# A two-layer diffusion backbone on one core: adaLN bias on rows, feed-forward sums added from PSUM, and the odd mixer's output product begun inside its last attention

## The chip, the cores and the metric

The kernel runs on one core of a Trainium2 chip. The metric is device time in microseconds, lower being better. A core has five engines that run in parallel, each through its own list of instructions in order: TensorE (PE, matrix products and transposes into PSUM), VectorE (DVE), ScalarE (ACT), GpSimd (POOL) and SyncE (SP, which here only issues DMAs). They wait for one another by semaphores.

## The reference

512 latent tokens and 256 context tokens, model width 1024, go through two layers. Each layer is a mixer and a gated feed-forward network, each with adaLN around it and a LayerNorm behind its residual sum:

```python
mod = (c_act @ mod_w[li] + mod_b[li])          # and modc for the context
sh_a, sc_a, g_a, sh_f, sc_f, g_f = jnp.split(mod, 6, -1)
h = x * (1 + sc_a) + sh_a
y = even_mixer(h, hc, ...) if li % 2 == 0 else odd_mixer(h, hc, ...)
x = layer_norm(DEEP_ALPHA * x + g_a * y, ln_g[li, 0], ln_b[li, 0])
hf = x * (1 + sc_f) + sh_f
x = layer_norm(DEEP_ALPHA * x + g_f * conv_ffn(hf, ...), ln_g[li, 1], ln_b[li, 1])
# even mixer's end
dn  = rms_norm(o_dn) * norm_w * silu(z)        # 4 gated DeltaNet heads
ret = group_norm(o_ret) * silu(g)              # 4 retention heads
y = concat([dn, ret]) @ w_out
# odd mixer's end, 8 heads of differential attention
o = rms_norm(softmax(q1 k1) v - lam * softmax(q2 k2) v) * subln_w * (1 - lambda_init)
y = merge_heads(o) @ w_out
```

The context passes through layer 0 with its own modulation; in layer 1 only the latent tokens are carried on.

## The kernel before

Tokens lie on partitions in tiles of 128: four of latent tokens (0 to 3) and two of context (4, 5). To keep float32 accuracy each product is three matmuls, of a high and a low part of either side: xh·wh, xh·wl, xl·wh. A weight comes in *units* of 1024 x 256 (`unit`, L174): SP loads it into `raw` (two buffers), ACT copies the high part `whi` (L147), and POOL or DVE, by `lo_engs`, subtracts to get `wlo` (L148). `raw` multiplied by a gate (L185) is POOL's, too.

A scheduler turns the program into one list per engine, by data dependences and by priority numbers: work written under a large number (`LATE`, 200) fills gaps; `pin` keeps an instruction at its place in program order. Buffers are reused through pools, and an instruction waits until its buffer is free.

The stages in order: the modulation of group 0 and the start; the DeltaNet phase, into which side work is laid (projections of later heads by `fill_unit`, and the adaLN products `mod_group_g`, one step each `SIDE` = 20 ticks); the retention phase (`ret_phase`), in which sums `wacc` of the even output product already run, head by head; `out_proj_ln(l=0)`; `ffn(0)`; the odd mixer; `out_proj_ln(l=1)`; `ffn(1)`.

What the change touches:

- `mod_group_g` multiplies in two halves of eight steps and copies the sum `mod_ps` to `modr` (L367), transposes it (`modt_ps`) and adds the bias `modbT` in columns (L375). `gate_rows` (L1223) reads a gate as rows from memory and adds a row of `mod_b` on POOL (L1232).
- `L1055` scales a DeltaNet head's `o_dn` by its rms `y` and the norm weight `nw`, on DVE, six times for each of four heads.
- In `ret_phase` heads' `kT` are copied by ACT (L1122), and the last head's `hTl` (L1108) is on DVE, behind the split of the last two units.
- At the end of `ffn(0)` each of six tiles gets two halves: gate product `gt` on DVE (L1425), sum into `acc` on POOL or DVE (L1559), LayerNorm, and `hTl` (L148) for the odd mixer.
- The odd mixer takes its heads in four pairs. In `attend` four blocks of queries per head give scores `sc`, probabilities `pt` (L1701, L1709), transposes `aT_ps` and `oall`; each head ends with rms and scaling by `sub` on DVE (L1731). Between, `project` for the next pair is laid in as filling; its rotary sums `otok` (L1618) are on POOL and are transposed by PE into `oT_ps`. In the last pair the filling is `sums` over heads 0 to 5, for tiles 0 and 1 and the first 512 columns, in the PSUM accumulators `accs`; the other two tiles' accumulators start behind the attention.
- `out_proj_ln(l=1)` loads x into `lx`, applies the LayerNorm weights that layer 0 left out (L1358 on DVE, L1359 on POOL), and adds the sums (L1380, L1381, L1383).

## Time and profile before

| | |
|---|---|
| median of three runs | 2055.08 us (2047.45 to 2055.61) |
| the profiled execution | 2056.78 us, of which the trace spans 2055.0 |
| PE busy in it | 1940.2 us, 94% of the span |
| DVE, ACT, POOL busy | 1199.5, 721.6, 765.1 us |
| mean granted clock of PE | 0.975 of full speed |

PE's share tells how much can be gained by any order of the same products; the list of its waits tells where. The clock that was granted to PE is told for each stretch: 1.00 is 2.4 GHz, 0.50 is 1.2 GHz.

### The profile page before, as it was taken

Reading aid. Unit: us, or ns where it says so; the run is one execution under the profiler, and the core shown is the slowest. Engines: PE = TensorE matmul, PEld = TensorE weight load, DVE = VectorE, ACT = ScalarE, POOL = GpSimd, SP = SyncE. Lnnn points to the kernel's source line nnn. Section 1 sums busy time; section 2 is a strip of 40 time slices with the busy share of each in tenths; the row PEclk is TensorE's granted clock in tenths of the full one; section 3 lists DMA queues with packets and bytes.
Section 4 is the critical chain, followed back from the end, with each engine's and each line's share of the span. In section 5 each row is a group of like instructions: output and inputs, shape, how many; then the busy total and the mean of one; then the engine's idle time right before and its main releaser. Section 6 shows DMA issues by size and latency. Waiting matters only on the chain. (4 is left out here: it accounts for less than half of the span.)

```text
span 2055.0 us, 33529 instructions
## 1 busy us (share of the span) xinstructions
PE 1940.2 (94%) x13766; PEld 1674.1 (81%) x13766; DVE 1199.5 (58%) x2452; ACT 721.6 (35%) x1295; POOL 765.1 (37%) x416
## 2 busy tenths in 40 slices
PE   7998999999899999999999998999997989999997
PEld 5877777778888888888888887989886888888886
DVE  3334744443467685666665657366667687656557
ACT  4432343423334432222222225354554444323221
POOL 1232322122422244544454434122213027656571
PEclk9999999999899999999999999999998999999999
DMA  9455344455614231111111112010102233323221
GB/s 290 137 168 163 111 128 141 122 163 181 195 47 164 83 103 62 62 62 62 62 62 62 62 62 90 22 42 30 54 32 78 77 121 126 102 83 103 82 82 41
DMA packets 198113, 201.33 MB, mean 98 GB/s; under 512 B 21336, under 2 KB 186808, under 8 KB 197960
## 3 DMA queue, kind: packets, MB, share of 16 engines
q1 hardware_dynamic: 195832, 196.78, 30.6%
q10 hardware_dynamic: 2128, 2.41, 0.4%
q8 instruction: 108, 1.77, 0.4%
q14 instruction: 45, 0.37, 0.1%
HBM read 185.89 MB, written 13.27 MB: 97 GB/s over the span
## 5 line engine op out<-in xcount | busy, mean ns | idle before, releaser
L148 POOL TENSOR_TENSOR wlo<-raw,whi 128x512 fp32r<-128x512 f32 (+2 forms) x158 | 413.9, 2642 | 487.6 <-ACT whi L147 442.5
L1476 DVE SCALAR_TENSOR_TENSOR ac<-g_ps,fconvT,ac 128x441 f32<-128x441 f32 (+2 forms) x352 | 243.9, 694 | 200.6 <-ACT ac L1465 190.9
L147 ACT CAST whi<-raw 128x2048 fp32r<-128x2048 f32 (+2 forms) x183 | 201.3, 1137 | 389.7 <-issue 247.4
L115 PE MATMUL d_ps<-whi,hh 128*128 128x512 f32 x440 | 173.3, 394 | 5.1 <-DVE gt L1425 4.4
L115 PE MATMUL d_ps<-wlo,hh 128*128 128x512 f32 x440 | 172.2, 391 | 0.0
L115 PE MATMUL d_ps<-whi,hl 128*128 128x512 f32 x440 | 171.6, 391 | 0.0
L115 PE MATMUL opj<-whi,hTh 128*128 128x256 f32 x512 | 147.1, 287 | 2.1 <-ACT oq L1629 1.6
L115 PE MATMUL g_ps<-hTl,whi 128*128 128x512 f32 (+1 forms) x384 | 145.2, 378 | 3.2 <-POOL hTl L148 3.2
L115 PE MATMUL opj<-whi,hTl 128*128 128x256 f32 x512 | 145.9, 285 | 0.0
L115 PE MATMUL opj<-wlo,hTh 128*128 128x256 f32 x512 | 145.1, 283 | 0.0
L115 PE MATMUL g_ps<-hTh,whi 128*128 128x512 f32 (+1 forms) x384 | 144.7, 377 | 0.0
L115 PE MATMUL u_ps<-hTh,whi 128*128 128x512 f32 (+1 forms) x384 | 144.6, 377 | 0.0
L115 PE MATMUL u_ps<-hTh,wlo 128*128 128x512 f32 (+1 forms) x384 | 144.6, 377 | 0.0
L115 PE MATMUL u_ps<-hTl,whi 128*128 128x512 f32 (+1 forms) x384 | 144.5, 376 | 0.0
L115 PE MATMUL g_ps<-hTh,wlo 128*128 128x512 f32 (+1 forms) x384 | 144.4, 376 | 0.0
L115 PE MATMUL fpj<-whi,hTh 128*128 128x256 f32 x432 | 127.1, 294 | 1.1 <-ACT fo L717 1.1
L115 PE MATMUL fpj<-wlo,hTh 128*128 128x256 f32 x432 | 126.7, 293 | 0.0
L115 PE MATMUL fpj<-whi,hTl 128*128 128x256 f32 x432 | 125.2, 290 | 0.0
L115 PEld LDWEIGHTS d_ps<-whi,hh 128*128 128x128 f32 x440 | 82.6, 188 | 26.1 <-DVE gt L1425 7.3
L115 PEld LDWEIGHTS opj<-whi,hTh 128*128 128x128 f32 x512 | 97.5, 191 | 4.2 <-ACT oq L1629 2.6
L1425 DVE TENSOR_TENSOR gt<-d_ps,gate 128x512 f32<-128x512 f32 x120 | 81.7, 686 | 29.7 <-PE d_ps L115 28.8
L115 PE MATMUL c_ps<-hTh,wlo 128*128 128x256 f32 x352 | 98.9, 281 | 0.0
(461 smaller groups left out, 4989.4 us busy)
## 6 DMA issues: line engine op xcount, KB each, us to landing
mraw<-in_mod_w_dram SPq DMA_DIRECT2D x80, 512.0 KB
raw<-in_f_w_gate_dram SPq DMA_DIRECT2D x22, 1024.0 KB
raw<-in_f_w_up_dram SPq DMA_DIRECT2D x22, 1024.0 KB
raw<-in_f_w_down_dram SPq DMA_DIRECT2D x22, 1024.0 KB
raw<-in_o_w_qkv_dram SPq DMA_DIRECT2D x12, 1024.0 KB
raw<-in_e_w_in_dram SPq DMA_DIRECT2D x9, 1024.0 KB
mraw<-in_mod_w_dram SPq DMA_DIRECT2D x32, 256.0 KB
raw<-in_e_w_in_dram SPq DMA_DIRECT2D x8, 512.0 KB
```

Of the source, the lines that this page charges most:

```text
L115: self.nc.tensor.matmul(out, lhsT=lhsT, rhs=rhs, start=start, stop=stop)
L147: self.nc.scalar.copy(h, r)
L148: lo_eng.tensor_sub(l, r, h.bitcast(F32))
L1425: v.tensor_mul(gt, ps, gates[0 if t < NLT else 1][:, n * 512:(n + 1) * 512])
L1476: v.scalar_tensor_tensor(out=o, in0=pv[:, r0 + di:r1 + di, c0 + dj:c1 + dj], scalar=cw[(di + 1) * 3 + dj + 1], in1=o, op0=ALU.mult, op1=AL ...
```

## The change

*adaLN bias.* `SIDE` becomes 18. `mod_group_g` loads four rows of `mod_b`, each spread over 32 partitions, into `modr` ahead of its second half, and adds the product to it from PSUM. The gates that go to memory then hold their bias, and `gate_rows` only loads.

*Even mixer's end.* `nw` is a column; it goes into the first four 128-row blocks of w_out when the unit is split (`unit_out`), and `o_dn`'s scaling is an ACT instruction. The split of the first two units comes after the first retention head's first step; that head's `kT` copies are on DVE.

*First feed-forward end.* The gate product is written back to PSUM, and DVE adds it from there, for all twelve halves. `cparts = 4` stands around the odd mixer's first two units. The projections' plain copies in `fill_unit` use another buffer for tile 2.

*Odd mixer.* x with the postponed LayerNorm weights is made in 16 pieces of 64 columns, during pairs 0 to 2, with two places for a piece (`xa` with `gb`, and `gate0`): loads one attention step ahead, two POOL instructions, a store. All four w_out units are scaled on POOL by gate rows that hold the subln weight. Head scaling is on ACT, the rms chain stays in PSUM. In the last pair `early` sums heads 0 to 5 for all eight blocks (four tiles, two halves) and adds each to ALPHA·x; only heads 6 and 7 are left for the end, which is now written in `odd_mixer` itself.

```diff
-SIDE = 20
+SIDE = 18
...
+    def unit_out(self, src, raw=None, pin=lambda ins: ins):
...
+        for sl, w in ((slice(0, n), self.nw[:, 0:1]), (slice(n, 2 * n), 1.0)):
+            pin(nc.scalar.activation(hi[:, sl], raw[:, sl], AF.Copy, scale=w))
+            pin(nc.vector.scalar_tensor_tensor(out=lo[:, sl], in0=raw[:, sl], scalar=w, in1=hi[:, sl].bitcast(F32),
+                                               op0=ALU.mult, op1=ALU.subtract))
...
+                if (hf, k) == (1, 0):
+                    for j in range(4):
+                        b = a["mod_b"][l, (4 * g + j) * 512:(4 * g + j + 1) * 512]
+                        nc.sync.dma_start(out=modr[32 * j:32 * j + 32, :], in_=b.partition_broadcast(32))
...
-        nc.vector.tensor_copy(modr, ps)
+        nc.vector.tensor_add(modr, ps, modr)
+        yield
...
-            v.scalar_tensor_tensor(out=od, in0=od, scalar=y[:, c:c + 1], in1=self.nw, op0=ALU.mult, op1=ALU.mult)
+            s_.activation(od, od, AF.Copy, scale=y[:, c:c + 1])
...
-                    s_.copy(t[:, grp[0] * P:(grp[-1] + 1) * P], ps[:, :len(grp) * P])
+                    (s_.copy if h or key == "q" else v.tensor_copy)(
+                        t[:, grp[0] * P:(grp[-1] + 1) * P], ps[:, :len(grp) * P])
...
-            self.pin(self.nc.gpsimd.tensor_add(t, t, gb))
...
+                if in_place:
+                    v.tensor_mul(ps, ps, gates[0 if t < NLT else 1][:, n * 512:(n + 1) * 512])
+                if gated or in_place:
                     return acc[t][:, n * 512:(n + 1) * 512], ps
...
-                            (v if n or not key else g).tensor_add(o, o, gt)
+                            v.tensor_add(o, o, gt)
...
+                        s_.activation(oall[:, t, hc], oall[:, t, hc], AF.Copy, scale=r[:, t:t + 1])
...
+                def early(heads):
+
+                    for n in range(2):
+                        for t in range(NLT):
+                            ps = pj.tile([P, 512], F32, tag="wo", name="wo_ps")
+                            with self.priority(LATE):
+                                for h in heads:
+                                    self.out_part([(t, ps)], us[2 * n:2 * n + 2], h, h == heads[-1])
...
+                                for o, c0, n_ in rest(t, n):
+                                    v.scalar_tensor_tensor(out=o, in0=o, scalar=ALPHA, in1=ps[:, c0:c0 + n_],
+                                                           op0=ALU.mult, op1=ALU.add)
...
+                def x_affine(i):
+
+                    cs = slice(i * 64, (i + 1) * 64)
+                    xp, gp = px[(i + 1) % 2]
+                    for j, op in enumerate((g.tensor_mul, g.tensor_add)):
+                        self.pin(op(xp, xp, gp[:, j].unsqueeze(1).to_broadcast([P, NLT, 64])))
+                    nc.sync.dma_start(out=self.xd[2][:LAT, cs].rearrange("(t p) n -> p t n", p=P), in_=xp)
...
+                    if 0 < i <= 16:
+                        x_affine(i - 1)
+                    if i < 16:
+                        x_load(i)
...
+                    if i == 20:
+                        scale(0)
+                        gate_rows_scale(xaf)
+                    if i == 21:
+                        split(0)
...
+                    if i == 23:
+                        scale(1)
+                        scale(2)
...
+                        fill = early(range(6))
...
+                            for h in (6, 7):
+                                self.out_part([(t, ps)], us[2 * n:2 * n + 2], h, h == 7, first=6)
+                            for o, c0, n_ in rest(t, n):
+                                v.tensor_add(acc[t][:, n * 512 + c0:n * 512 + c0 + n_], ps[:, c0:c0 + n_], o)
```

Three places show what this does to the order of work. First, DVE at the even mixer's last head, where `hTl` is what PE's last sums wait for. Before:

```order
L136 SCALAR_TENSOR_TENSOR rs_y<-rs_w,rs_y 128x6
L1207 TENSOR_TENSOR gvar<-gmv,rs_y 128x6
L1208 TENSOR_SCALAR gvar<-gvar 128x6
L148 TENSOR_TENSOR wlo<-raw,whi 128x1024 x4
L1108 TENSOR_TENSOR hTl<-yT_ps,hTh 128x256
L1108 TENSOR_TENSOR hTl<-yT_ps,hTh 128x512
L1385 TENSOR_TENSOR gy<-wacc,gate_7254 128x512 x2
L1386 SCALAR_TENSOR_TENSOR gy<-lx,gy 128x512 x2
```

After:

```order
L149 SCALAR_TENSOR_TENSOR rs_y<-rs_w,rs_y 128x6
L1253 TENSOR_TENSOR gvar<-gmv,rs_y 128x6
L1254 TENSOR_SCALAR gvar<-gvar 128x6
L1152 TENSOR_TENSOR hTl<-yT_ps,hTh 128x256
L1152 TENSOR_TENSOR hTl<-yT_ps,hTh 128x512
L1396 TENSOR_TENSOR gy<-wacc,gate_7266 128x512
L222 SCALAR_TENSOR_TENSOR wlo<-raw,nw,whi 128x1024
L222 SCALAR_TENSOR_TENSOR wlo<-raw,whi 128x1024
```

The two `hTl` and a gate product have moved ahead of the four splits `wlo`.

Second, POOL in the odd mixer's pairs 0 to 2, where `otok` is the rotary sum, `wlo` the split of a unit, and `xa` and `gate` are the two places for pieces of x. Before:

```order
L1618 TENSOR_TENSOR otok<-otok,ob 128x512 x4
L148 TENSOR_TENSOR wlo<-raw,whi 128x2048
L1618 TENSOR_TENSOR otok<-otok,ob 128x512 x2
L148 TENSOR_TENSOR wlo<-raw,whi 128x2048
L1618 TENSOR_TENSOR otok<-otok,ob 128x512 x2
L148 TENSOR_TENSOR wlo<-raw,whi 128x2048 x2
L1618 TENSOR_TENSOR otok<-otok,ob 128x512 x2
```

After, the corresponding first half:

```order
L1634 TENSOR_TENSOR otok<-otok,ob 128x512 x4
L161 TENSOR_TENSOR wlo<-raw,whi 128x2048
L1634 TENSOR_TENSOR otok<-otok,ob 128x512 x2
L1805 TENSOR_TENSOR gate_12984<-gate_12984 128x256
L161 TENSOR_TENSOR wlo<-raw,whi 128x2048
L1805 TENSOR_TENSOR gate_12984<-gate_12984 128x256
L1634 TENSOR_TENSOR otok<-otok,ob 128x512
L1805 TENSOR_TENSOR xa<-xa,gb 128x256 x2
L1805 TENSOR_TENSOR gate_12984<-gate_12984 128x256 x2
L1805 TENSOR_TENSOR xa<-xa,gb 128x256 x2
L1805 TENSOR_TENSOR gate_12984<-gate_12984 128x256
L1634 TENSOR_TENSOR otok<-otok,ob 128x512
```

The pieces, in pairs of instructions, stand between the splits and the rotary sums.

Third, DVE at the odd mixer's end, behind the last head's rms. Before, `hTl` for heads 6 and 7 stands behind the scaling of `oall`, and the affine of `lx` among the sums:

```order
L136 SCALAR_TENSOR_TENSOR rs_y<-rs_w,rs_y 128x4
L1731 SCALAR_TENSOR_TENSOR oall<-oall,rs_y,sub 128x128 x4
L1741 TENSOR_TENSOR hTl<-yT_ps,hTh 128x512 x2
L1380 TENSOR_TENSOR gt<-wo_ps,gate_15588 128x512 x2
L1358 TENSOR_TENSOR lx<-lx,lng 128x1024
L148 TENSOR_TENSOR wlo<-raw,whi 128x1024
L1358 TENSOR_TENSOR lx<-lx,lng 128x1024 x2
L1381 TENSOR_TENSOR lx<-gt,lx 128x512
L1358 TENSOR_TENSOR lx<-lx,lng 128x1024
L1254 BN_STATS lst<-lx 128x6
L1381 TENSOR_TENSOR lx<-gt,lx 128x512
L1383 TENSOR_TENSOR lx<-wo_ps,lx 128x512
```

After, with the late ones of the early sums (L1769) among the sums of heads 6 and 7 (L1914):

```order
L131 SCALAR_TENSOR_TENSOR rs_y<-rs_w,aT_ps 128x4
L1756 TENSOR_TENSOR hTl<-yT_ps,hTh 128x512
L1914 TENSOR_TENSOR oall<-wo_ps,oall 128x512
L1291 BN_STATS lst<-oall 128x6
L1914 TENSOR_TENSOR oall<-wo_ps,oall 128x256
L1769 SCALAR_TENSOR_TENSOR oall<-oall,wo_ps 128x256
L1914 TENSOR_TENSOR oall<-wo_ps,rest 128x256
L1769 SCALAR_TENSOR_TENSOR rest<-rest,wo_ps 128x256
L1291 BN_STATS lst<-oall 128x6
```

The scaling of `oall` and the affine of x have left this place; two halves of an early sum still stand in it.

## Rows read from the trace of the kernel before

**Rows 1.** the page's head: span, busy time of each engine (share of span, instructions).

```profile
span 2055.0 us, 33529 instructions
...
PE 1940.2 (94%) x13766; PEld 1674.1 (81%) x13766; DVE 1199.5 (58%) x2452; ACT 721.6 (35%) x1295; POOL 765.1 (37%) x416
```

**Rows 2.** PE's waits: tile, line, waited for: us in total, times, longest.

```profile
PE ln_ps L119 <- ACT acc L1274: 9.7, 6, 4.3
PE wo_ps L115 <- DVE hTl L1741: 7.4, 1, 7.4
...
PE mod_ps L115 <- DMA mraw<-in_mod_w_dram: 6.0, 4, 3.3
PE wo_ps L115 <- DVE lx L1383: 5.2, 1, 5.2
PE wacc L115 <- DVE hTl L1108: 4.8, 1, 4.8
PE modt_ps L119 <- DVE modr L367: 4.6, 3, 3.3
...
PE rT_ps L119 <- ACT kT L1122: 3.0, 1, 3.0
...
PE oT_ps L119 <- POOL otok L1618: 3.0, 8, 1.0
```

**Rows 3.** windows: start:end, length, busy us (instructions) by engine, PEclk, DMA share, GB/s.

```profile
516.20:523.00 6.80, 5.83 (x28) 5.84 (x29) 2.30 (x10) 2.08 (x9) 1.34 (x4) 0.50 0.58 192
...
635.70:642.50 6.80, 3.72 (x17) 3.72 (x18) 5.92 (x9) 0.00 (x0) 0.00 (x0) 0.50 0.79 253
1267.10:1270.50 3.40, 2.98 (x14) 2.98 (x15) 0.54 (x1) 2.79 (x6) 3.40 (x1) 0.51 0.47 186
1567.50:1570.90 3.40, 3.40 (x17) 3.26 (x17) 3.37 (x6) 1.50 (x3) 2.33 (x1) 0.50 0.92 291
1574.30:1584.60 10.30, 4.32 (x18) 4.13 (x19) 7.55 (x11) 5.36 (x7) 6.87 (x2) 0.50 0.00 0
1618.70:1622.10 3.40, 3.40 (x19) 3.40 (x17) 0.43 (x1) 0.59 (x1) 0.00 (x0) 0.50 0.00 0
1652.80:1659.70 6.90, 5.84 (x27) 5.84 (x28) 6.90 (x18) 1.87 (x3) 0.00 (x0) 0.51 0.00 0
```

**Rows 4.** DVE instructions by line: shortest/median/longest in ns, first and last start.

```profile
L1055 DVE SCALAR_TENSOR_TENSOR o_dn<-o_dn,rs_y,nw x24: 343/346/4637, 278.7 to 511.1; 128x128 f32<-128x128 f32 x24
...
L148 DVE TENSOR_TENSOR hTl<-hf,hTh x16: 674/682/3515, 664.9 to 1679.9; 128x512 fp32r<-128x512 f32 x16
...
L1731 DVE SCALAR_TENSOR_TENSOR oall<-oall,rs_y,sub x32: 337/346/4544, 1359.9 to 1626.8; 128x128 f32<-128x128 f32 x32
...
L148 DVE TENSOR_TENSOR wlo<-raw,whi x25: 691/1220/3410, 11.2 to 1690.2; 128x1024 fp32r<-128x1024 f32 x18, 128x2048 fp32r<-128x2048 f32 x4, 128x512 fp32r<-128x512 f32 x3
```

**Rows 5.** timeline, DVE and POOL: start, us, instruction, [idle before, releaser].

```profile
509.83 5.96 DVE L1055 SCALAR_TENSOR_TENSOR o_dn<-o_dn,rs_y,nw 128x128 f32<-128x128 f32 x6
...
510.92 4.72 POOL L148 TENSOR_TENSOR wlo<-raw,whi 128x2048 fp32r<-128x2048 f32 x1 [4.55 <-ACT whi L147]
...
629.40 8.99 DVE L148 TENSOR_TENSOR wlo<-raw,whi 128x1024 fp32r<-128x1024 f32 x4 [4.48 <-POOL o_ret L1099]
...
629.33 5.71 POOL L1232 TENSOR_TENSOR gate<-gate,gy 128x1024 f32<-128x1024 f32 x2
...
1256.40 4.60 POOL L148 TENSOR_TENSOR wlo<-raw,whi 128x2048 fp32r<-128x2048 f32 x1 [0.42 <-ACT whi L147]
...
1568.58 8.99 POOL L185 TENSOR_TENSOR raw<-raw,gate 128x2048 f32<-128x2048 f32 x2 [11.64 <-DMA raw<-in_o_w_out_dram]
```

**Rows 6.** windows as in group 3: one pair of heads, and the odd end.

```profile
1366.00:1447.00 81.00, 78.71 (x608) 74.39 (x608) 48.78 (x106) 39.53 (x79) 18.79 (x7) 0.98 0.12 40
...
1562.00:1670.00 108.00, 88.14 (x638) 83.39 (x637) 84.35 (x162) 45.28 (x89) 31.06 (x9) 0.89 0.26 85
```

**Rows 7.** POOL's groups by shape: busy us, mean ns, idle before and releaser.

```profile
L713 POOL TENSOR_TENSOR fo<-fo,fb 128x256 f32<-128x256 f32 x16 | 11.9, 744 | 40.3 <-DVE fb L712 27.0 <-issue 5.7 <-DMA XZ<-gdr 4.0
```

More of the change, by code (lines that the diff above doesn't have):

```diff
@@ L174, in unit, with unit_load @@
     def unit(self, parts, scale=None):
+        raw = self.unit_load(parts)
+        if scale is not None:
+            self.unit_scale(raw, scale)
+        return self.unit_split(raw)
+    def unit_load(self, parts):
         nc = self.nc
@@ L296, in setup @@
         nc.vector.memset(self.onescol, 1.0)
+        self.nw = cp.tile([P, 1], F32, name="nw")
+        nc.scalar.dma_start(out=self.nw, in_=a["e_norm_w"][0].rearrange("(p o) -> p o", o=1))
         self.lneps = cp.tile([P, 1], F32, name="lneps")
@@ L1131, in ret_phase @@
         w_out = a["e_w_out"][0]
-        self.lo_engs = "v"
-        units = [self.unit([w_out[:, u * 256:(u + 1) * 256]]) for u in range(2)]
+        raws = [self.unit_out_load(w_out[:, u * 256:(u + 1) * 256]) for u in range(2)]
         accs = {t: accp.tile([P, 512], F32, tag="wo", name="wacc") for t in (4, 5, 0, 1)}
         gens = [head(h) for h in range(HEADS)]
+        units = None
         for step in "0 1 a 0 0 2 b 0 1 1 3 c 1 2 d 2 e 2 3 f 3 3 g h".split():
@@ L1139, in ret_phase @@
                 next(gens[int(step)], None)
+                units = units or [self.unit_out(None, r) for r in raws]
             else:
@@ L1221, in row, with gate_rows @@
         return t
-    def gate_rows(self, pool, l, which, streams, gb=None):
-        if gb is None:
-            gb = self.rawp.tile([P, 8 * 256], F32, tag="raw", name="raw")[:, :D]
-        self.nc.sync.dma_start(
-            out=gb, in_=self.a["mod_b"][l, (2 + 3 * which) * D:(3 + 3 * which) * D].partition_broadcast(P))
-        gates = []
-        for s in range(streams):
-            t = self.row(pool, self.gd[l][which][s], f"gate{s}")
-            self.pin(self.nc.gpsimd.tensor_add(t, t, gb))
-            gates.append(t)
-        return gates
+    def gate_rows(self, pool, l, which, streams):
+        return [self.row(pool, self.gd[l][which][i], f"gate{i}") for i in range(streams)]
     def affine_rows(self, pool, l, which):
@@ L1320, in h_tiles, with out_part @@
             self.split(hf, self.hT[0][:, ks, sl], self.hT[1][:, ks, sl], nc.gpsimd if kq % 2 else nc.vector)
-    def out_part(self, accs, units, k, last):
+    def out_part(self, accs, units, k, last, first=0):
         yh, yl = self.hT
@@ L1330, in out_part, with out_proj_ln @@
                     self.mm(ps[:, u * 256:(u + 1) * 256], xi[:, k, ts], wi[:, k, :],
-                            start=(k == 0 and u == 0 and j == 0), stop=(last and u == 1 and j == 2))
-    def out_proj_ln(self, l, w_out, key, src, xh, groups, accp, accs, us, trp, gates=None):
+                            start=(k == first and u == 0 and j == 0), stop=(last and u == 1 and j == 2))
+    def out_proj_ln(self, w_out, key, xh, groups, accp, accs, us, trp):
         nc = self.nc
         with ExitStack() as st:
-            lnp = self.pool(st, f"lnA{l}")
-            pp = accp if l == 0 else self.pool(st, f"ps_wout{l}", bufs=2, space=PSUM)
-            self.ln_pools(st, f"lnA{l}", trp=trp)
+            lnp = self.pool(st, "lnA0")
+            self.ln_pools(st, "lnA0", trp=trp)
@@ new lines, in gate_rows_scale, with load, scale, split @@
+                def gate_rows_scale(t):
+                    self.pin(g.tensor_scalar_mul(t, t, sub[:, 0:1]))
+                def load():
+                    u = len(raws)
+                    raws.append(self.unit_load([w_out[:, u * 256:(u + 1) * 256]]))
+                def scale(u):
+                    self.pin(self.unit_scale(raws[u], gates[u]))
+                def split(u):
+                    us.append(self.unit_split(raws[u]))
+                def step(i):
+                    if 0 < i <= 16:
+                        x_affine(i - 1)
+                    if i < 16:
+                        x_load(i)
+                    if i == 17:
+                        gate_load(gate, 0, 512)
+                        gates[:2] = gate[:, :256], gate[:, 256:]
+                    if i == 18:
+                        gate_rows_scale(gate)
+                        load()
+                    if i == 19:
+                        gate_load(xaf, 512, 256)
+                        gates[2] = xaf
+                    if i == 20:
[3 more added lines that the diff above has]
+                        split(0)
+                        load()
+                    if i == 22:
+                        load()
+                    if i == 23:
+                        scale(1)
+                        scale(2)
+                    if i == 25:
+                        gate_rows_scale(gates[3])
+                        scale(3)
+                    if i == 26:
+                        split(3)
+                        for t in range(NLT):
+                            nc.sync.dma_start(out=end[:, t, :], in_=self.x_src(3, t)[:, 768:])
```

202 lines of the change are left out of this document (111 added, 91 removed).

## The prediction

> **What bounds the kernel now.** The page comes first: TensorE (PE) is busy 1940.2 of 2055.0 us [rows 1]. The change keeps every product of three matmuls, so it can win only PE's idle time (2055.0 − 1940.2 = 114.8 us) and the time that PE loses at half clock. The list of PE's waits says where PE stands and for whom [rows 2]: most of the entries are DVE or ACT results at the joints between stages, each 3 to 7 us long. The third view is a table of short windows in which the granted clock reads 0.50 [rows 3], the lower of the two levels (1.2 instead of 2.4 GHz). Each of them holds or follows one of those waits. A matmul takes twice as long there, so a window costs half of its PE busy time on top of the wait. A removed wait is therefore worth its own length and, if PE then stays busy, half of the busy time in the window behind it.
>
> Why DVE is late is seen by laying its instructions beside those of POOL (GpSimd). The same DVE instruction has a usual and an extreme length: o_dn at L1055 346 against 4637 ns, hTl at L148 682 against 3515 ns, oall at L1731 346 against 4544 ns [rows 4]. The long ones stand where POOL runs a wide tensor-tensor: o_dn x6 takes 5.96 us from 509.83 under the wlo of 510.92; wlo x4 takes 8.99 us from 629.40 under the gate sums of 629.33; the scaling of raw (8.99 us from 1568.58) covers the oall rows and the wlo of 1256.40 the hTl [rows 4, 5]. All these DVE instructions read two large operands from SBUF; in this trace the copies out of PSUM and the reductions beside them keep their length. So the change is to be judged by which DVE instruction it takes off PE's path and which POOL instruction it puts beside others.
>
> The Trainium skill, "SBUF — State Buffer", section "Who interferes with whom", states that a DVE instruction with two SBUF inputs contends with a GpSimd instruction reading SBUF, for whole instructions. The long rows [rows 4, 5] agree; what follows from it for this change is the third rival.
>
> **The change, part by part**, against the profiled execution, 2056.78 us (span 2055.0 and 1.8 around it; it lies 1.7 above the median of 2055.08).
>
> (a) The o_dn scaling goes from DVE to ACT, the norm weight into the rows of w_out. The 5.96 us of DVE delay the copy modr, for which PE waits 3.3 us [rows 2]; the window behind it has 5.83 us busy at half clock, 2.9 lost [rows 3]. On ACT six short scalings remain, behind which modr no longer stands. The split of w_out on DVE keeps its two large operands and its size. Gain 3.3 + 2.9 = **6.2** (bounds 0 and 6.2).
>
> (b) At the even out-projection the last head's hTl now stands ahead of the four wlo on DVE, and the two gate sums on POOL (5.71 us) are gone, their bias having come in with mod's rows. PE's wait of 4.8 us goes, and 3.72/2 = 1.9 of clock [rows 2, 3]. Next late is the wlo itself: four at their usual 1.22 us [rows 4], needed only when the third and fourth unit begin, behind the sums already queued; I charge 1. Gain 4.8 + 1.9 − 1 = **5.7** (bounds 0 and 6.7).
>
> (c) At the first feed-forward end all twelve sums are DVE tensor-tensors that read PSUM, POOL's six adds go, and the gate product stays in PSUM. The longest ln_ps wait, 4.3 us with 2.98/2 = 1.5 of clock [rows 2, 3], came from hTl stretched to 3.52 under POOL's wlo and an add behind it. The twelve sums cost DVE six more instructions of about 0.7 us (hTl's usual 682 ns is the nearest row with such operands), spread over three groups of tiles. I charge 0.8. Gain **5.0** (bounds −3 and 5.8).
>
> (d) The first retention head's kT copies move to DVE: PE waits 3.0 us for them once [rows 2]. DVE has work there too; I take **2** (0 to 3).
>
> (e) The odd end. In 1562 to 1670 PE is busy 88.14 of 108 us [rows 6]: 19.9 idle, 7.4 of it for hTl behind the stretched oall scalings, 5.2 for lx behind the affine of x [rows 2]. The four half-clock windows hold 3.40, 4.32, 3.40 and 5.84 us of PE, half of 16.96 being 8.5 [rows 3]. Gross 28.4. The change takes off both causes: oall's scaling is on ACT (busy 39.53 of 81 us in a pair [rows 6]), x and its affine are ready before the last pair, and early sums of heads 0 to 5 give PE work inside the last attention; behind it only heads 6 and 7 remain. What comes back: the first early sum needs units 0 and 1, whose scaling and lo wait on POOL behind two scalings of 4.5 us each (8.99 for two [rows 5]) while only attention fills PE, I take 4; the last tile's LayerNorm now has fewer products in front of it, and the ln_ps waits, 9.7 in six [rows 2], say 1.6 each for two tiles, 3; with those, clock loss of half the 6 us or so behind them, 3. Gain 28.4 − 10 = **18.4** (bounds 2, where only the tail's lx wait less a new bubble is left, and 28.4).
>
> (f) mod work one step per 18 ticks instead of 20, its bias as four row loads per group. The steps' matmuls are the same, only earlier; PE's waits for mraw are 6.0 us in four [rows 2]. They could go or double: **0** (−6 to +6).
>
> (g) New POOL work in pairs 0 to 2: 16 pieces of x with two instructions of 744 ns [rows 7], 23.8 us. Room there is: POOL is busy 18.79 of 81 us in such a pair [rows 6]. But POOL works in order, and in the whole new order 6 of the rope sums (otok) stand directly behind a piece or a gate scaling. PE's transposes oT_ps already wait for POOL 8 times, 3.0 us in all [rows 2], so a later otok has little slack. Six at about 1 us (between none and one piece, 1.49): **+6** (bounds 0 and 66, see the second rival). SP, too, gets four DMAs per piece, ahead of which nothing of PE's is waiting while DMA is busy 0.12 there [rows 6]; nothing charged. The Trainium skill, "DMA: Bandwidth & Descriptors", section "Specifications", wants at least 512 bytes per transfer for line rate, and a piece has 256; by that the pieces would land later, but with the queues that empty it changes no term unless the wait reaches POOL.
>
> Sum: −6.2 − 5.7 − 5.0 − 2 − 18.4 + 0 + 6 = −31.3, so 2056.8 − 31.3 = **2025.5**, taken as 2026.
>
> **Rivals.** First, the odd end gives nothing: the early sums are starved by POOL and the bubble at LayerNorm costs what the attention saved. For it: POOL's three scalings (4.5 us each) and splits (wlo, 4.60) around the last pair's start [rows 5]; against it: 7.4 and 5.2 us were waits for work that is gone. Without (e) the sum is −13, time 2044; with the low end 2 it is 2042.
>
> Second, **slower**: POOL's order couples PE to the landing of x. Each piece waits for its own loads and, being in order, holds the rope sum behind it, and that holds PE's transposes, for which there is no other work. If a piece lands late, each of 14 rope sums in the pairs costs 3 us for the landing and 1.7 for the pieces, 66 us instead of 6, and the time is 2056.8 − 31.3 + 60 = 2086. It decides from about 37/14 = 2.6 us per rope sum on, where the other parts are eaten up. Against it: a piece is loaded one attention step ahead, some 81/8 = 10 us, with the DMA idle for nine tenths [rows 6].
>
> Third, DVE stays stretched: hTl of the feed-forward end, the w_out splits and the affine sums of the odd end still read two SBUF operands while POOL keeps its wide wlo. This is what the skill's rule would give. Then (c) gains nothing (−5.0), (b) half (−2.8) and the odd end loses one such stretch, about 3.5: −31.3 + 11.3 = −20, time 2037.
>
> Fourth, everything works with no new idle time: (e) gives 28.4 and (g) costs 0: −47, time 2010.
>
> **How the numbers follow.** A difference below about 0.5% (10 us) can't be told from none. Chances: forecast (2016 to 2034) 0.46, third rival (2034 to 2040) 0.16, first rival (2040 to 2050) 0.16, fourth (2003 to 2016) 0.12, slower 0.06, and 0.04 for a stall that no row hints at. The cases between 2016 and 2050 make up 0.78, the fourth's upper half brings it over 0.8: range 2008 to 2050. The first rival is split at 2045: faster by over 0.5% 0.82, within 0.5% 0.11, slower 0.07.
>
> **What will show it.** Right would be: the waits for modr and for the even mixer's last hTl gone, no half-clock window near 517, 636 and 1267; oall's scaling absent from DVE; PE busy over 95% from the last pair to the next g_ps; oT_ps waits below 10 us in all. Wrong would be: oT_ps waits for otok of over 2 us each (second rival), g_ps or wo_ps waiting for POOL's wlo in the last pair (first), DVE's hTl still at 3 us and more near the feed-forward end (third). The sum fails most easily in (e): more than half of the forecast hangs on a stage whose new waits no row of before shows.

## The result, and the profile after

The changed kernel takes 2024.2 us (median of 4 runs, 2021.63 to 2025.54) against 2054.61 us for the kernel before beside it: a ratio of 0.9869, 95% interval 0.985 to 0.9888. Forecast were 2026 us in a range of 2008 to 2050. The profiled execution took 2025.01 us, 31.8 less than the one before.

The head of the page answers to [rows 1]; the second line is the count of DMA packets, of which 21336 were under 512 B before.

```profile
span 2023.2 us, 33715 instructions
...
PE 1919.7 (95%) x13765; PEld 1657.4 (82%) x13765; DVE 1164.0 (58%) x2398; ACT 731.3 (36%) x1353; POOL 778.2 (38%) x445
...
DMA packets 220483, 204.59 MB, mean 101 GB/s; under 512 B 43400, under 2 KB 209304, under 8 KB 220328
```

PE is busy 20.5 us less, although its products are the same: most of that is clock (the granted mean rose from 0.975 to 0.986). Idle time fell by 11.3 us. PE's waits, in the columns of [rows 2], tell where:

```profile
PE oT_ps L119 <- POOL otok L1634: 8.6, 9, 3.7
...
PE wo_ps L115 <- ACT hTh L1755: 5.8, 1, 5.8
...
PE mod_ps L115 <- DVE modT L419: 5.3, 2, 3.0
PE rT_ps L119 <- ACT qT L1166: 4.9, 1, 4.9
...
PE ln_ps L119 <- ACT acc L1311: 3.0, 4, 1.1
PE ln_ps L119 <- DVE hf L1351: 3.0, 2, 2.7
...
PE modt_ps L119 <- DVE modr L413: 1.8, 1, 1.8
```

The entries for hTl in both layers and for lx are gone, modt fell from 4.6 to 1.8 us, and ln_ps <- acc from 9.7 to 3.0. New are wo_ps <- ACT hTh (5.8), mod_ps <- DVE modT (5.3 in two, at 256 and 345 us) and rT_ps <- ACT qT (4.9, in place of kT's 3.0); oT_ps <- otok grew from 3.0 to 8.6. The half-clock windows of [rows 3] have gone at 517, 636 and 1574. The one at 1267, 11 us behind the first projection of the odd mixer, has a successor 7 us behind it, at 1244, and more stand in the odd mixer now:

```profile
1244.10:1247.50 3.40, 3.40 (x19) 3.40 (x18) 3.40 (x8) 0.24 (x1) 3.40 (x2) 0.51 0.76 263
1353.40:1356.80 3.40, 3.40 (x19) 3.40 (x17) 0.98 (x2) 2.11 (x6) 3.40 (x1) 0.50 0.33 77
1435.30:1442.10 6.80, 5.00 (x24) 5.00 (x25) 0.98 (x2) 2.41 (x6) 6.80 (x4) 0.50 0.34 78
1561.60:1568.40 6.80, 3.92 (x18) 3.92 (x19) 1.46 (x4) 5.07 (x9) 4.79 (x2) 0.50 0.02 5
```

Where the 31.8 us went is read by cutting both traces at the same instructions of PE: the first product, the first rT_ps (start of retention), the first wacc (even output product), the first g_ps (feed-forward), the first scores sc behind it (odd attention), the last opj (odd projections), the next g_ps, and the last product. The first scores are taken as a cut, and not the first opj, because the same 3444 instructions of PE lie between g_ps and them in both kernels; ahead of the first opj the changed kernel has 12 transposes of the LayerNorm (ln_ps) fewer, which have moved behind it. The rows are windows from one cut to the next, first of before, then of after; the columns are those of [rows 3].

```profile
3.56:549.99 546.43, 508.91 (x5167) 416.69 (x5168) 245.07 (x751) 194.96 (x442) 149.20 (x116) 0.96 0.55 164
549.99:562.07 12.08, 8.07 (x49) 6.86 (x47) 5.77 (x10) 6.42 (x13) 4.06 (x3) 0.72 0.49 154
562.07:686.73 124.66, 115.75 (x942) 111.38 (x940) 87.82 (x244) 52.30 (x94) 33.76 (x18) 0.97 0.32 102
686.73:1314.96 628.23, 611.44 (x3447) 528.91 (x3446) 382.38 (x605) 171.96 (x249) 275.80 (x146) 1.00 0.20 67
1314.96:1558.00 243.04, 233.93 (x1819) 219.88 (x1818) 150.11 (x314) 125.08 (x249) 54.36 (x21) 0.99 0.12 40
1558.00:1669.87 111.87, 91.67 (x661) 86.28 (x660) 87.21 (x165) 48.79 (x92) 31.06 (x9) 0.89 0.25 81
```

```profile
4.37:539.81 535.44, 498.75 (x5165) 406.59 (x5166) 238.17 (x722) 198.08 (x464) 147.70 (x116) 0.98 0.56 167
539.81:552.76 12.95, 7.26 (x43) 5.96 (x41) 6.15 (x10) 5.66 (x12) 5.74 (x3) 0.74 0.77 242
552.76:671.79 119.03, 113.71 (x947) 109.64 (x946) 83.10 (x247) 51.59 (x93) 28.71 (x17) 1.00 0.32 100
671.79:1296.27 624.48, 611.80 (x3447) 529.94 (x3445) 392.83 (x611) 173.09 (x255) 264.24 (x144) 1.00 0.20 67
1296.27:1543.30 247.03, 234.95 (x1820) 221.07 (x1819) 137.97 (x287) 130.85 (x269) 95.47 (x58) 0.98 0.22 61
1543.30:1637.67 94.37, 85.84 (x655) 79.72 (x653) 63.23 (x153) 49.01 (x100) 19.08 (x5) 0.96 0.22 73
```

| stage | before | after | difference | forecast, by term |
|---|---|---|---|---|
| start and DeltaNet | 546.4 | 535.4 | -11.0 | -6.2 (a), 0 (f) |
| into retention | 12.1 | 13.0 | +0.9 | -2 (d) |
| retention, even output product | 124.7 | 119.0 | -5.6 | -5.7 (b) |
| first feed-forward, first projections | 628.2 | 624.5 | -3.7 | -5.0 (c) |
| odd pairs, from the first scores on | 243.0 | 247.0 | +4.0 | +6 (g) |
| odd end | 111.9 | 94.4 | -17.5 | -18.4 (e) |
| second feed-forward | 372.3 | 372.6 | +0.3 | 0 |

The stage numbers agree so well that the reasons behind them had to be tested one by one; some of them fell. Two cautions. The second and third row are best read together, since 6 instructions of PE have moved across the cut between them (49 against 43 in the short stage): 136.7 us became 132.0, -4.8 where -7.7 was forecast. And for the first stage: up to the last product of the DeltaNet inverse (m_ps) it took 453.1 us before and 448.8 after, but 445.0 to 452.4 in runs of the changed kernel in which nothing there was touched. Of its -11.0 only the rest is read as the change: from that product to the first rT_ps 93.4 us became 86.6, that is -6.8. The other stages took, in executions of the changed kernel whose edits stand elsewhere, 130.5 to 133.0 us (the two rows together), 622.7 to 625.8 (first feed-forward), 245.5 to 247.9 (odd pairs) and 94.3 to 95.1 (odd end).

### The profile page after: what moved, and what is told of

Read it like the earlier page. It is cut to its first block, busy times and chain, and to the rows that moved or that the text cites. A ratio compares the mean times of both kernels' runs of the same rounds, so it can differ in the third digit from the quotient of the medians.

```text
span 2023.2 us, 33715 instructions
## 1 busy us (share of the span) xinstructions
PE 1919.7 (95%) x13765; PEld 1657.4 (82%) x13765; DVE 1164.0 (58%) x2398; ACT 731.3 (36%) x1353; POOL 778.2 (38%) x445
## 2 busy tenths in 40 slices
DMA packets 220483, 204.59 MB, mean 101 GB/s; under 512 B 43400, under 2 KB 209304, under 8 KB 220328
## 5 line engine op out<-in xcount | busy, mean ns | idle before, releaser
L161 POOL TENSOR_TENSOR wlo<-raw,whi 128x512 fp32r<-128x512 f32 (+2 forms) x166 | 426.2, 2595 | 496.7 <-ACT whi L160 464.1
L160 ACT CAST whi<-raw 128x512 fp32r<-128x512 f32 (+2 forms) x183 | 194.5, 1099 | 400.7 <-issue 237.2
L115 PE MATMUL fpj<-wlo,hTh 128*128 128x256 f32 x432 | 122.5, 284 | 0.0
L115 PE MATMUL c_ps<-hTl,whi 128*128 128x256 f32 x352 | 99.0, 281 | 0.0
```

Of the source, the lines that this page charges most:

```text
L115: self.nc.tensor.matmul(out, lhsT=lhsT, rhs=rhs, start=start, stop=stop)
L160: self.nc.scalar.copy(h, r)
L161: lo_eng.tensor_sub(l, r, h.bitcast(F32))
```

## Experiments

Times are medians, ratios are against the kernel before as it ran beside each set of runs; its medians were 2049.6 to 2054.6 us, so that between sets ratios compare better than times (the changed kernel: 0.9869). "Stage" is a row of the table above, cut in the same way.

### Who removed the wait for modr: four runs

The changed kernel with o_dn's scaling back on DVE:

```diff
-            s_.activation(od, od, AF.Copy, scale=y[:, c:c + 1])
+            v.scalar_tensor_tensor(out=od, in0=od, scalar=y[:, c:c + 1], in1=self.onesq, op0=ALU.mult, op1=ALU.mult)
```

> The changed kernel (2024 us) with the scaling of o_dn back on DVE, as an instruction with two large SBUF operands (the second one a tile of ones, since the norm weight stays folded in w_out). Theory A, as predicted in (a): the move to ACT is what took the wait away; the scaling stretches again under POOL's wlo, modr comes late, PE waits some 3 us and has a half-clock window behind it: +5 to +6 us, 2030. Rival B: with a mod step per 18 ticks modr is written near 494 us, ahead of the last head's scaling, so nobody on PE's path stands behind it any more: the scaling may stretch, and the time stays within 1 us of 2024.

Measured: 2025.08 us, ratio 0.9853 (0.9829 to 0.9876). Rival B holds: nothing on PE's path stood behind the scaling, which came at 513 us, 19 us after modr. It did not stretch either, since POOL's wlo (4.62 us from 506.21) had ended by then, so this run says nothing on the stretching:

```profile
513.11 1.67 DVE L1101 SCALAR_TENSOR_TENSOR o_dn<-o_dn,rs_y,onesq 128x128 f32<-128x128 f32 x6
```

The changed kernel with the old spacing:

```diff
-SIDE = 18
+SIDE = 20
```

> The changed kernel with SIDE back at 20 and o_dn's scaling still on ACT. Theory A (the move to ACT counts, the spacing is worth nothing): no wait at modt near the end of the DeltaNet phase, within 2 us of 2024. Rival B (the spacing counts): the last mod steps fall again near 511 us, behind which the retention phase starts, and the time rises by 4 to 8 us, 2028 to 2032.

Measured: 2034.4 us, ratio 0.9906 (0.9885 to 0.9928): 10 us over the changed kernel by the medians, 7.6 by the ratios, at or above the upper end of rival B. From the last m_ps to the feed-forward's first g_ps the traces show 227.3 us against 218.6. Each group of mod work has one step more than before (the added `yield`), 17 instead of 16; five groups make 85 steps, which at 20 ticks want 1700 ticks where 80 steps wanted 1600. The last group is not done when the filling ends, and PE waits 5.0 us for its weights, at 525 us:

```profile
PE mod_ps L115 <- DMA mraw<-in_mod_w_dram: 7.9, 5, 5.0
```

So the spacing of 18, by this count, first of all pays for the added step: 85 times 18 is 1530. No run leaves the step out. The spacing has a price, too: the waits of mod_ps for modT (5.3 us in the changed kernel) are absent here.

The kernel before with either edit alone (the second leaves the norm weight out):

```diff
-SIDE = 20
+SIDE = 18
```

> The kernel before (2055 us) with SIDE 18 and nothing else. Theory B (where the last mod step falls decides, found with the two runs on the changed kernel): the copy modr comes ahead of the last o_dn scaling, PE's 3.3 us wait at modt and the 2.9 us of clock behind it go: -5 to -8 us, about 2048. Theory A (the scaling on ACT is needed): the wait stays or moves, 2053 to 2057.

```diff
-            v.scalar_tensor_tensor(out=od, in0=od, scalar=y[:, c:c + 1], in1=self.nw, op0=ALU.mult, op1=ALU.mult)
+            s_.activation(od, od, AF.Copy, scale=y[:, c:c + 1])
```

> The kernel before with o_dn's scaling as an ACT instruction and SIDE still 20; the norm weight is left out, so that one part of the computation is missing and no other instruction changes. Theory A: modr no longer stands behind a stretched scaling, PE's 3.3 us wait and its clock window go: -5 to -6 us, about 2049. Rival: another DVE or ACT instruction is late there, or the clock window stays: 0 to -3 us.

Measured: with the spacing alone 2054.29 us, ratio 1.0023 (1.0004 to 1.0042); with the scaling on ACT alone 2044.5 us, ratio 0.9964 (0.9945 to 0.9982). From the last m_ps to the first rT_ps the two take 87.4 and 86.8 us, where the kernel before took 93.4: either edit removes the wait of 3.3 us for modr. But both give most of it back at the next joint, where PE waits for the copy of kT on ACT, 3.0 us before:

```profile
PE rT_ps L119 <- ACT kT L1122: 7.5, 1, 7.5
...
PE rT_ps L119 <- ACT kT L1122: 6.7, 1, 6.7
```

From the first rT_ps to the feed-forward's g_ps the two take 143.9 and 142.4 us, where the kernel before took 136.7 and the changed kernel 132.0. What follows: two edits that the prediction counted apart are substitutes for one wait, and alone they gain next to nothing at these joints. The 7.4 us of the second (2051.86 to 2044.5) are clear of noise all the same, and most of them lie elsewhere: up to the last m_ps its trace takes 444.8 us against 453.1. Whether the scaling on ACT shortens that phase, which scatters by 7 us among executions, is open.

What keeps the gain in the changed kernel is seen on ACT, whose copies stand behind fo, the copy of a filling projection, which waits for a store to leave its buffer. In the kernel before with the spacing alone, and in the changed kernel:

```profile
552.14 0.72 ACT L717 COPY fo<-fpj 128x256 f32<-128x256 f32 x2 [8.31 <-DMA rvd<-fo]
555.13 0.37 ACT L717 COPY fo<-fpj 128x256 f32<-128x256 f32 x1 [2.27 <-DMA rvd<-fo]
...
557.20 0.86 ACT L1122 COPY kT<-rT_ps 128x256 f32<-128x256 f32 x2
...
544.64 0.37 ACT L761 COPY fo<-fpj 128x256 f32<-128x256 f32 x1 [7.72 <-DMA rvd<-fo]
544.91 0.38 ACT L761 COPY fb<-fpj 128x256 f32<-128x256 f32 x1
...
546.49 0.38 ACT L1166 COPY qT<-rT_ps 128x256 f32<-128x256 f32 x1
```

From the first of these fo to the copy that PE waits for it takes 5.1 us there and 1.9 here: tile 2 has a buffer of its own (fb) and does not wait for a second store, and whi is copied in halves. The move of kT to DVE lets PE do six more transposes first, and it then waits for qT. So the gain may be owed to the buffer as much as to (d); no run has either alone.

### Order or contention at the even output product: two runs

```diff
-            us = [us, [self.unit_out(w_out[:, u * 256:(u + 1) * 256], pin=self.pin) for u in (2, 3)]]
+            us = [us, [self.unit_out(w_out[:, u * 256:(u + 1) * 256]) for u in (2, 3)]]
```

> The changed kernel without the pin on the split of the third and fourth unit of the even output product: DVE has the four wlo ahead of the last head's hTl again, as before the change, while POOL's two gate sums stay away. Theory A (order counts): PE waits for hTl behind four wlo of 1.22 us each, 2 to 4 us, and loses 1 to 2 us to a half-clock window: +3 to +6. Rival B (POOL's sums made the wait by stretching the wlo): the four take their usual 4.9 us, which the sums in progress cover: +0 to +1.

```diff
             gates = self.gate_rows(lnp, 0, 0, 2)
+            zr = lnp.tile([P, D], F32, name="zr")
+            nc.vector.memset(zr, 0.0)
+            for t in gates:
+                self.pin(nc.gpsimd.tensor_add(t, t, zr))
```

> The changed kernel with POOL's two gate sums of 128x1024 back (a row of zeros is added), and hTl still ahead of the wlo on DVE. Theory A (order counts): the wlo stretch from 5 to some 9 us behind hTl, and are wanted later; +0 to +2. Rival B (POOL's sums count): PE waits again near 4 us at the last head: +4 to +6.

Measured: 2025.03 us, ratio 0.9855 (0.9833 to 0.9878), and 2028.3 us, ratio 0.9881 (0.9855 to 0.9907). The stage took 118.3 us with the old order and no sums, 120.1 with the new order and the sums, 119.0 in the changed kernel, 124.7 before. So neither edit taken back brings the wait back; with the short stage ahead of it the two runs have 130.7 and 132.7 us, inside the scatter of 130.5 to 133.0. (The second run's median lies 4 us over the changed kernel's, as rival B had it, but in its trace 3.6 of them stand ahead of the last m_ps.) The timeline of DVE in the first of the two shows why:

```profile
622.11 1.28 DVE L222 SCALAR_TENSOR_TENSOR wlo<-raw,nw,whi 128x1024 fp32r<-128x1024 f32 x1 [4.49 <-POOL o_ret L1143]
...
625.64 1.22 DVE L222 SCALAR_TENSOR_TENSOR wlo<-raw,whi 128x1024 fp32r<-128x1024 f32 x1
626.77 1.02 DVE L1152 TENSOR_TENSOR hTl<-yT_ps,hTh 128x256 fp32r<-128x256 f32 x2
```

The four wlo stand ahead of hTl as before, but take 4.8 us in all instead of the 8.99 of [rows 5], and hTl is done before PE runs out of sums. In the second run POOL's sums and the wlo don't meet at all:

```profile
624.32 4.75 POOL L1384 TENSOR_TENSOR gate<-gate,zr 128x1024 f32<-128x1024 f32 x2
...
629.72 1.28 DVE L222 SCALAR_TENSOR_TENSOR wlo<-raw,nw,whi 128x1024 fp32r<-128x1024 f32 x1
```

With hTl first, the wlo begin when the sums are over, and keep their 1.28 us. So this run does not test contention behind hTl, as it was meant to; it shows that the new order takes the wlo out from under the sums. (b) was near in size and half right in its reason: either half of it would have been enough, the bias on rows, which took POOL's sums away, or the order. That the old wait needed both is the kernel before itself; no run puts both back into the changed kernel.

### The first feed-forward end: two runs

```diff
-                            o, gt = down(ws[1], xs[1], t, n, ps, first=False, gated=not key, in_place=key)
-                            v.tensor_add(o, o, gt)
+                            o, gt = down(ws[1], xs[1], t, n, ps, first=False, gated=not key)
+                            (v if n or not key else g).tensor_add(o, o, gt)
```

> The changed kernel with the first feed-forward end as before: gate product into SBUF, the first half's sum on POOL. Theory (c): +4 to +5 us, with a ln_ps wait of about 4 us near 1245 us of the span. Rival: the wait there comes from hTl stretched under POOL's wide wlo, which the change has not removed (hTl 3.74 us, a ln_ps wait of 2.7 us in the changed kernel): 0 to +2.

Measured: 2034.31 us, ratio 0.9913 (0.9882 to 0.9944). The stage is 629.7 us, 5.2 over the changed kernel's, and the long ln_ps wait is back:

```profile
1248.17 0.69 PE L119 MATMUL ln_ps<-ident,acc 128*128 128x128 f32 x2 [4.33 <-ACT acc L1311]
```

(c) holds. (The median is 10 us over the changed kernel's; the traced execution, the shortest of the four at 2027.57 us, shows no more than these 5.) What it left, as the third rival said, is an hTl stretched to 3.74 us under POOL's wide wlo, with 2.7 us of ln_ps <- hf. The last of the twelve runs cuts those wlo into four (it holds the four repairs of the section on the pieces too):

```diff
+                self.cparts = 4
                 for _ in project(0, ((4, 0), (2,)), nxt):
                     pass
+                self.cparts = 1
```

> The same as the four repairs, and the splits that run while the first feed-forward end writes its last hTl are in four parts of 512 columns on POOL instead of one of 2048. Theory (third rival of the prediction): hTl on DVE, 3.74 us there under a POOL subtraction of 4.8, can be held up by 1.3 us at most, and the ln_ps wait of 2.7 us goes: the stage from the first g_ps to the first opj shrinks by 2 to 4 us. If POOL's instructions follow one another without a gap that lets DVE in, it stays: 0.

Measured: 2019.9 us, ratio 0.9849 (0.9823 to 0.9874); the stage took 624.9 us, not less. The reason is seen on DVE, POOL and PE:

```profile
1234.39 1.28 DVE L161 TENSOR_TENSOR hTl<-hf,hTh 128x512 fp32r<-128x512 f32 x1
...
1238.32 0.68 DVE L161 TENSOR_TENSOR hTl<-hf,hTh 128x512 fp32r<-128x512 f32 x1
...
1246.77 4.69 DVE L161 TENSOR_TENSOR hTl<-hf,hTh 128x512 fp32r<-128x512 f32 x1 [0.98 <-ACT hTh L160]
...
1232.40 2.73 POOL L161 TENSOR_TENSOR wlo<-raw,whi 128x512 fp32r<-128x512 f32 x2 [5.16 <-ACT whi L160]
...
1246.35 4.56 POOL L161 TENSOR_TENSOR wlo<-raw,whi 128x2048 fp32r<-128x2048 f32 x1 [4.22 <-issue]
...
1252.16 0.66 PE L119 MATMUL ln_ps<-ident,acc 128*128 128x128 f32 x4 [3.62 <-DVE hf L1351]
```

Beside two pieces of 512 columns, from 1232.40 to 1235.13, hTl takes 1.28 us; with POOL idle, at 1238.32, its usual 0.68. But one wlo of 2048 columns, from the unit behind those that were cut, now starts 0.4 us ahead of another hTl, which takes 4.69 us and ends 0.55 behind it, and PE waits 3.6. So the mechanism is confirmed on one and the same line, and the repair missed: all wide POOL subtractions near that end would have to go, which no run tries. The Trainium skill, "SBUF — State Buffer", section "Who interferes with whom", states that a DVE instruction with two SBUF inputs contends with a GpSimd instruction that reads SBUF, and that the port pair they share is an exclusive lock; the 4.69 us beside the 4.56 of wlo agree with that.

### The pieces of x: two runs

```diff
-                    if 0 < i <= 16:
-                        x_affine(i - 1)
-                    if i < 16:
-                        x_load(i)
```

with x loaded as it was left in memory (`x_src(2, t)`), so that the postponed weight and bias are left out.

> The changed kernel without the 16 pieces: no loads, POOL instructions and stores for them; the last layer's x is then taken without the postponed LayerNorm weight and bias, which leaves that part of the computation out. Theory (g): the pieces cost what the pairs grew by, 4 us, in two waits of PE for otok (2.7 and 3.7 us) with half-clock windows behind: -4 to -8 us, and the pairs as long as before. Rival: the pairs grew for another reason (order of the projections), -1 to +1.

Measured: 2014.01 us, ratio 0.982 (0.9791 to 0.9848), 10 us under the changed kernel. The pairs take 235.4 us instead of 247.0. So the pieces cost 11.6 us, twice the 6 of term (g), and something else in the change had shortened the pairs, by 7.6 us against the 243.0 before and by 6.2 against the 241.6 of the two other executions that have the old pairs (the kernel before with either edit alone), for which the prediction has no term. Of the 11.6 us 5.4 are idle time, and 4.2 are half of the 8.40 us that PE was busy in the windows at 1353 and 1435; without the pieces the clock of the stage is 1.00. How a piece costs PE time, in the changed kernel on DVE, POOL and PE, and POOL's group of them:

```profile
1428.97 0.75 DVE L1632 TENSOR_TENSOR ob<-opj,ca 128x256 f32<-128x256 f32 x2
...
1433.62 1.52 POOL L1805 TENSOR_TENSOR xa<-xa,gb 128x256 f32<-128x256 f32 x2 [4.80 <-DMA xa<-xd]
...
1435.79 1.26 POOL L1634 TENSOR_TENSOR otok<-otok,ob 128x512 f32<-128x512 f32 x1
...
1437.10 1.11 PE L119 MATMUL oT_ps<-ident,otok 128*128 128x128 f32 x4 [3.71 <-POOL otok L1634]
...
L1805 POOL TENSOR_TENSOR xa<-xa,gb 128x256 f32<-128x256 f32 x16 | 11.8, 736 | 20.6 <-DMA xa<-xd 19.9
```

DVE had the rope sum's operand (ob) ready at 1429.7. POOL sat idle for 4.8 us until the piece ahead of it had landed, worked 2.2 us on that piece and half of the next, and the sum came 6 us late; PE waited 3.7. In all POOL waited 19.9 us for pieces in xa. That is the second rival's mechanism, mostly at 2 of the 14 rope sums (PE waits 2.7 and 3.7 us) instead of all.

The repair kernel puts two attention steps instead of one between a piece's load and its POOL instructions (`x_affine(i - 2)`), and makes three more edits in other stages:

```diff
-        nc.scalar.dma_start(out=self.nw, in_=a["e_norm_w"][0].rearrange("(p o) -> p o", o=1))
...
+        nc.sync.dma_start(out=self.nw, in_=a["e_norm_w"][0].rearrange("(p o) -> p o", o=1))
...
-                    (s_.copy if h or key == "q" else v.tensor_copy)(
+                    (s_.copy if h else v.tensor_copy)(
...
-                    s_.copy(yh, ps)
+                    (v.tensor_copy if h == 5 else s_.copy)(yh, ps)
...
-                    if 0 < i <= 16:
-                        x_affine(i - 1)
+                    if 1 < i <= 17:
+                        x_affine(i - 2)
```

> The changed kernel with four repairs of waits that its trace shows, each in a stage of its own. Pieces of x are loaded two attention steps ahead instead of one: if the landing is what holds POOL and the rope sums behind it, the pairs shrink by 4 to 8 us; if POOL's own time does, by 0 to 2. The norm weight's column is loaded later, not first on ACT's queue: the first product comes 2 us sooner. The first retention head's qT copies on DVE too: the 4.9 us wait for ACT goes, -4. The high part of the sixth head on DVE, not behind ACT's copy of a unit that waits for POOL's scaling: the 5.8 us wait goes, -5 to -7. In all -12 to -18: 2006 to 2012.

Measured: 2022.18 us, ratio 0.9863 (0.9837 to 0.9888): no difference from the changed kernel that can be told. Edit by edit: the pairs took 242.7 us, 4.3 less (243.8 in the kernel with the cut wlo, 3.3 less), at the lower edge of the first theory; the wait behind one of the two late sums fell from 2.7 to 1.1 us, the other stayed at 3.2, since POOL still waits for a landing, 4.65 us at 1434.60:

```profile
1434.60 1.52 POOL L1805 TENSOR_TENSOR gate<-gate 128x256 f32<-128x256 f32 x2 [4.65 <-DMA gate<-xd]
```

A place is loaded again only after its store, and the edit moves the store one step later, too: SP waited 16.6 us in all for stores before it could issue loads of x, 14.5 in the changed kernel. The first lat came at 18.4 us instead of 20.3, and at 19.4 in the kernel with the cut wlo, which has this edit too, where the runs without it had 19.6 to 20.7: 0.2 to 2.3 us. The wait for qT (3.4 to 5.1 us in the runs that have it) became one for the next head's kT of 4.9 us, and the wait for hTh stayed (6.2 us). Both had been read one step short:

```profile
546.18 0.37 ACT L761 COPY fo<-fpj 128x256 f32<-128x256 f32 x1 [7.76 <-DMA rvd<-fo]
...
1562.05 1.90 ACT L160 CAST whi<-raw 128x2048 fp32r<-128x2048 f32 x1 [6.01 <-POOL raw L207]
1563.85 0.58 ACT L1755 CAST hTh<-yT_ps 128x512 fp32r<-128x512 f32 x1
```

In the first case ACT waits 7.8 us for the store of a filling projection (fo) to leave its buffer, and any copy behind it is late. In the second ACT's queue holds whi, the copy of a unit that POOL is still scaling (4.52 us from 1557.50), ahead of the fourth head's hTh; the repair moved the sixth head's.

### The odd end: two runs

```diff
-                        fill = early(range(6))
+                        fill, late = iter(()), early(range(6))
...
+                for _ in late:
+                    pass
                 for h in (6, 7):
                     to_y(h)
```

> The changed kernel with the early sums of heads 0 to 5 behind the last pair's attention instead of inside it; all products stay. Theory (e): the filling takes 24 us of PE into that attention, whose idle time it covers; without it the stage from the last projection to the feed-forward's first g_ps (94.4 us) grows by 10 to 20 us, most of it idle time of PE inside the attention and half-clock windows. Rival: the stage shrank because of the scaling on ACT and the ready x alone; it grows by 0 to 4 us.

Measured: 2028.93 us, ratio 0.9902 (0.9877 to 0.9926); the stage took 95.3 us, 1.0 more, and the rest of the longer time is spread over stages that the edit leaves alone. This does not decide for the rival, since the edit did not do what it was meant to do: the sums are written behind the attention, but the scheduler still put them into it. PE's wo_ps in the 60 us from about the last opj on, in the changed kernel and in this one:

```profile
1543.00:1603.00 60.00, 23.88 (x149) 20.31 (x149) 2.72 (x4) 0.94 0.26 90
...
1544.00:1604.00 60.00, 23.12 (x148) 19.92 (x148) 2.71 (x4) 0.94 0.27 91
```

148 matmuls stand in that window, where 149 did. What the filling is worth was not measured; a run that holds the sums back until the attention's end was not made.

```diff
-                        s_.activation(oall[:, t, hc], oall[:, t, hc], AF.Copy, scale=r[:, t:t + 1])
+                        v.scalar_tensor_tensor(out=oall[:, t, hc], in0=oall[:, t, hc], scalar=r[:, t:t + 1], in1=self.onesq,
+                                               op0=ALU.mult, op1=ALU.mult)
```

> The changed kernel with the head scaling of oall back on DVE, with two large SBUF operands (a tile of ones as the second; the subln weight stays in the gate rows). Without the pieces the pairs took 293.3 us, 8.7 less than before the change, which the prediction has no term for. Theory: this scaling on DVE, ahead of the reductions and probabilities of the next head, was what cost them; then the pairs grow by 5 to 9 us (306.3 to 311 to 315), and the last pair's stage by 1 to 4. Rival: the 8.7 us come from elsewhere (the rms chain in PSUM, the order), and the time stays within 2 us.

Measured: 2030.68 us, ratio 0.9908 (0.9879 to 0.9936). The pairs took 249.6 us, 2.5 more (1.7 over the highest of the untouched), the odd end 96.8, 2.4 more, with a new wait of 1.6 us for oall. So the scaling on DVE costs, but some 2.5 us in the pairs and not 6 to 8. PE's waits for ACT copies ahead of its projections (oq, ov), 2.1 us before and none without the pieces, are back with it at 1.8. Between the two other executions with the old pairs and the run without the pieces (6.2 us) PE's idle time differs by 2.5 us, 9.2 against 6.7: those 2.1 and 1.9 of sc waiting for pt on ACT less, 1.1 of aT_ps waiting for pt on DVE more. The other 3.7 us are PE busy longer with the same products, 232.4 against 228.7 us at a clock of 1.00 in both, and are not settled.

## Why the prediction was right, and where its steps were not

- **What bounds the kernel**: right. 11 of the 32 us are idle time of PE, most of the rest is clock; the windows at 517, 636 and 1574 vanished with the waits that they belonged to. Of its signs two did not come: a half-clock window still stands at the feed-forward's end (1244), and from the last opj to the next g_ps PE is busy 85.84 of 94.37 us, 91% and not over 95. Of the signs for rivals two came, the rope sums that PE waits for longer than 2 us and the long hTl.
- **(a) and (f)**: the size of the sum was right (-6.8 against -6.2), the assignment wrong. The prediction gave all to ACT and nothing to the spacing. Either would have done on the kernel before, and in the changed kernel it is the spacing: without it some 9 us are lost, by the count of steps to the added one. "The steps' matmuls are the same, only earlier" failed to count the steps: 85 instead of 80. The waits for mraw, which could go or double, went from 6.0 to 3.8 us, but 5.3 us for modT came.
- **(d)**: the wait did not go (+0.9 instead of -2); it became one for qT behind the same late ACT instructions. Both single edits wait 6.7 and 7.5 us at this place and the changed kernel 4.9; what of that is the move and what the buffer of its own for tile 2, for which the prediction has no term, is not shown.
- **(b)**: near in size (-5.6 against -5.7, but only -4.8 with the stage ahead of it); of the two causes that it named together either one removed was enough.
- **(c)**: right, 3.7 to 5.2 us, and the third rival was right in its premise: hTl stayed stretched at 3.74 us. They don't exclude each other, as the prediction had it: with the old end the wait is 4.3 us, with the new one 2.7, at an hTl of 3.50 and 3.74 us.
- **(g)**: mis-sized. The pieces, whose 32 instructions all stand between 1329.7 and 1452.3 us, in half of the stage's 247, cost 11.6 us, not 6: the landing of a piece was charged at nothing, and POOL waited 19.9 us for it; nor was the clock charged, 4.2 us behind the waits. The stage came out near the forecast because of 6 to 8 us for which it had no term.
- **(e)**: right in size, 17.5 of 18.4, though which of its parts (early sums, scaling on ACT, ready x) brought it is open but for the 2.4 us of the scaling. The new waits were one wait, 5.8 us for hTh with 2 us of clock behind it (3.92 us busy at half), from POOL's scaling, as the first rival had it; the bubble at LayerNorm, charged with 3 us, did not come: PE is busy 34.70 of the last 35 us of the stage.

Two errors of opposite sign in (g), and two in (a), (f) and (d), cancelled, and 4.2 of the 31.8 us stand ahead of the last m_ps, where only (f), charged at 0, could act and executions scatter by 7. That the total was right to 0.1% is in part luck; the terms were right to some 6 us each.

The Trainium skill, "DMA: Bandwidth & Descriptors", section "Specifications", gives 512 bytes as the least transfer for line rate; a piece's rows have 256. What the runs show is that packets under 512 B doubled from 21336 to 43400, and that a piece's landing is what POOL waits for. Whether their size makes them late, or the store that SP waits for ahead of a load (14.5 us in all), no run here tells apart.

## What to carry to other kernels

Where a wait stands at a joint, list everything that would come late next behind the same engine's queue: an edit that removes a wait alone can gain nothing (the spacing alone, 1.0023), and two edits can be substitutes. Work moved to an idle engine is not free if the engine runs in order and its input comes by DMA: the price here was the landing of the piece ahead, paid by the sum that stood behind it. An experiment that moves program text under a scheduler is read in the order of the instructions before its time is believed. And a stage is cut where the same instructions lie on either side: at the first opj 12 transposes had changed sides.

## What the runs showed of the hardware beyond the expected

- A DVE subtraction of two SBUF operands took 0.68 us with POOL idle, 1.28 beside POOL subtractions of 512 columns (two in 2.73 us) and 4.69 beside one of 2048 (4.56 us): with shorter instructions on POOL the delay was shorter.
- One DMA of 0.5 KB in 4-byte elements (nw), placed first on ACT's queue, went with a first product of the projections 2.3 us later than before (20.3 against 18.0 us); with it moved it came at 18.4 and 19.4.
- The phase up to the last m_ps varies between 445.0 and 452.4 us among executions that differ only behind it, more than most edits here are worth; the later stages vary by 1 to 3 us, so that a cut from the trace tells a change of 3 us or so that a whole run does not.
